# Row sums of 16,384 rows on one core: two blocks of rows for each partition, 112 and 16, laid out as one block of 128

## The chip, the core and the metric

The kernel runs on one core of a Trainium2 chip. The metric is the device time of an execution in microseconds (us). The profile is one execution that was recorded by the hardware profiler; its span runs from its first to its last recorded instruction or transfer.

## The reference

```python
def setup_inputs():
    batch, seq, dim = 32, 512, 1024
    return {"x": np.random.randn(batch, seq, dim).astype(np.float32)}

def reference(x):
    return np.sum(x, axis=-1).astype(np.float32)
```

There are 32 x 512 = 16,384 rows of 1,024 float32 numbers, 4 KB a row and 67.1 MB in all. The output is one float32 sum for each row, 64 KB. Every number is read once and added once.

## The kernel before

The rows are spread over the 128 partitions of the on-chip memory, 128 rows (C) for each partition. They come in two blocks of the input. The first 14,336 rows are the body: partition p has the 112 rows (BODY) that begin at row 112p. The other 2,048 rows are the end: partition p has 16 rows (G) that begin at row 14,336 + 16p. The inner function `block` (lines 27 to 30) makes the views for a block: `x_a` and `out_a` for the body, `x_z` and `out_z` for the end.

The body is loaded in seven steps of 16 rows a partition, 64 KB a partition and 8.39 MB a step, into three buffers `xt` in turn. The end uses the next buffer in turn and comes in pieces of 9, 4 and 2 rows (`CUTS`), and its last row comes in two parts of 544 and 480 columns into a tile of its own, `tail`. All loads are issued by SyncE on one queue, in the order of the list `loads` (lines 128 to 131). From the fourth step on, a load waits until VectorE has finished the step that used the buffer before. The first two loads are moved ahead into the program's entry block (lines 154 to 173); they are one row and fifteen rows of the first step, so that the first step is two DMAs.

VectorE sums 16 rows a step with one tensor_reduce (`rows_dve`, line 55) into `res_a`. In the seventh step it takes nine rows and ScalarE seven, one activation with an accumulator for each row (`rows_act`, line 66). In the end the two engines share the pieces. The last rows are summed on VectorE by instructions that add two halves of a row and accumulate (`pairs_dve`, line 73). The two parts of the last row follow one another, the second one taking up the sum of the first. The sums of the end go to `res_z`.

The results are stored by SyncE on the same queue as the loads. The store of `res_a` (line 135) is issued once the first part of the last row has landed, and the store of `res_z` (line 138) once every sum is there. SyncE then waits for both, clears the semaphores and ends:

```python
    nc.sync.dma_start(out=out_a, in_=res_a[:, :]).then_inc(sems["early_store"], 16)
    nc.sync.wait_ge(vec, count["vec"])
    nc.sync.wait_ge(act, count["act"])
    nc.sync.dma_start(out=out_z, in_=res_z[:, :]).then_inc(sems["store"], 16)
```

Of the kernel before, what the change touches and what calls it, by code (L numbers as in the profile page):

```python
# [9 lines left out]
BODY = 112  # L10
G = 16
# [7 lines left out]
def row_sums(nc, x: bass.AP, out: bass.AP):  # L19
    P = nc.NUM_PARTITIONS  # L20
    x_flat = x.flatten_outer_dims()
    R, D = x_flat.shape
    C = R // P
    assert R % P == 0 and C == BODY + G and BODY % G == 0
    out_flat = out.rearrange("a (b c) -> (a b c)", c=1)

    def block(r0, n):
        x_b = x_flat[r0 : r0 + P * n].rearrange("(p c) d -> p (c d)", p=P)
        out_b = out_flat[r0 : r0 + P * n].rearrange("(p c) -> p c", p=P)
        return x_b, out_b  # L30

    x_a, out_a = block(0, BODY)
    x_z, out_z = block(P * BODY, G)

    def sbuf(name, n):
        return nc.alloc_sbuf_tensor(name, [P, n], F32)
# [47 lines left out]
    for b in range(n_bufs):  # L84
        c = b * G
# [60 lines left out]
def kernel(tc: tile.TileContext, x: bass.AP, out: bass.AP):  # L146
    tc.close()
    tc.compile()  # L148
    nc = tc.nc
    row_sums(nc, x, out)  # L150

    sp = mybir.EngineType.SP
    fn = nc.m.functions[0]
    entry, body = None, None
    for blk in fn.blocks:
        ops = [i for i in blk.instructions if i.engine == sp]
        if entry is None:
            entry = blk  # L160
        elif any(i.opcode == "DMACopy" for i in ops):
            body = blk
            break
    code = list(body.instructions)
    loads = [i for i in code if i.engine == sp and i.opcode == "DMACopy"][:EARLY]
    for load in loads:
        assert not load.sync_info.on_wait
        code.remove(load)
    body.instructions = code
    code = list(entry.instructions)  # L170
    at = next(k for k, i in enumerate(code) if i.engine == sp and i.opcode == "Drain")
    code[at:at] = loads
    entry.instructions = code
# [29 lines left out]
```

## Time and profile before

| | |
|---|---|
| median of 3 runs | 160.55 us (160.54 to 160.86) |
| the profiled execution | 160.55 us |
| its span | 159.2 us |
| VectorE busy | 121.4 us (76% of the span), 16 instructions |
| ScalarE busy | 17.2 us (11%), 31 instructions |
| moved by the DMA queue | 67.18 MB, mean 422 GB/s |
| one reduce of 16 rows a partition | 17.2 us |
| store of `res_a`, 56 KB, issue to landing | 1.6 us |
| store of `res_z`, 8 KB, issue to landing | 1.4 us |

In the profile, DVE is VectorE, ACT is ScalarE, SPq is SyncE's queue of instructions, and "DMA" the 16 DMA engines. L55 is line 55 of the kernel. A part written out<-in names the tensor that is written and the one that is read, `in_x_dram` and `out_dram` being the input and the output in the chip's main memory. The rows of digits cut the span into 40 equal slices, with the busy share of each in tenths. In a timeline, the brackets hold the idle time of the engine before the instruction and what ended it. A packet is one contiguous run that a DMA engine moves, or the closing packet that counts up a semaphore.

### The profile page before, as it was taken

Reading aid. Unit: us, or ns where it says so; the run is one execution under the profiler, and the core shown is the slowest. Engines: PE = TensorE matmul, PEld = TensorE weight load, DVE = VectorE, ACT = ScalarE, POOL = GpSimd, SP = SyncE. Lnnn points to the kernel's source line nnn. Section 1 sums busy time; section 2 is a strip of 40 time slices with the busy share of each in tenths; the row PEclk is TensorE's granted clock in tenths of the full one; section 3 lists DMA queues with packets and bytes.
Section 4 is the critical chain, followed back from the end, with each engine's and each line's share of the span. In section 5 each row is a group of like instructions: output and inputs, shape, how many; then the busy total and the mean of one; then the engine's idle time right before and its main releaser. Section 6 shows DMA issues by size and latency. Waiting matters only on the chain.

```text
span 159.2 us, 107 instructions
## 1 busy us (share of the span) xinstructions
DVE 121.4 (76%) x16; ACT 17.2 (11%) x31; POOL 0.2 (0%) x4
## 2 busy tenths in 40 slices
DVE  0000059997799968999499994999949999499685
ACT  3000000000000000000000000000000000494694
POOL 0000000000000000000000000000000000000000
DMA  9988996996996999979969969969979899699994
GB/s 379 494 370 370 494 527 263 527 527 263 527 494 296 527 395 395 527 313 477 527 263 527 527 263 527 527 263 527 477 313 527 362 428 527 296 445 445 387 400 152
DMA packets 2160, 67.18 MB, mean 422 GB/s; under 512 B 496, under 2 KB 624, under 8 KB 880
## 3 DMA queue, kind: packets, MB, share of 16 engines
q1 hardware_dynamic: 2160, 67.18, 98.1%
HBM read 67.11 MB, written 0.07 MB: 422 GB/s over the span
## 4 chain that ended last, share of the span: by engine, by line
DMA 75%; DVE 22%; SPq 1%; issue 0%
DMA xt<-in_x_dram 50%; DMA tail<-in_x_dram 25%; DVE res_a L55 22%; SPq L131 1%; DVE pairs L73 0%; DVE res_z L73 0%
## 5 line engine op out<-in xcount | busy, mean ns | idle before, releaser
L55 DVE TENSOR_REDUCE res_a<-xt 128x16 f32<-128x16384 f32 (+1 forms) x7 | 113.1, 16153 | 32.3 <-DMA xt<-in_x_dram 32.3
L66 ACT ACTIVATE xt<-xt 128x1024 f32<-128x1024 f32 x15 | 15.6, 1043 | 138.1 <-DMA xt<-in_x_dram 138.1
L55 DVE TENSOR_REDUCE res_z<-xt 128x4 f32<-128x4096 f32 (+1 forms) x2 | 6.7, 3353 | 1.7 <-DMA xt<-in_x_dram 1.7
L66 ACT ACTIVATION_READ_ACCUMULATOR xt<-xt 128x1 f32 x15 | 2.8, 187 | 0.0
L97 DVE MEMSET tail<- 128x1 f32 x1 | 0.1, 59 | 2.0 <-PEq L148 2.0
L66 ACT ACT_TABLE_LOAD x1 | 1.3, 1283 | 1.9 <-PEq L148 1.9
L73 DVE CUSTOM_DVE_ANT_0 pairs<-tail 128x272 f32<-128x272 f32 (+1 forms) x2 | 0.9, 427 | 0.1
L73 DVE CUSTOM_DVE_ANT_0 pairs<-xt 128x512 f32<-128x512 f32 x1 | 0.7, 693 | 0.2 <-DMA xt<-in_x_dram 0.2
L73 DVE DVE_READ_ACCUMULATOR2_ANT res_z<- 128x1 f32 x2 | 0.2, 82 | 0.0
L187 POOL MEMSET const-uint8-127<- 128x1 uint8 x1 | 0.1, 102 | 0.0
L187 POOL MEMSET const-bfloat16-1.0<- 128x1 bf16 x1 | 0.1, 101 | 0.0
L187 POOL MEMSET const-float32-0.0<- 128x1 f32 x1 | 0.1, 98 | 0.2 <-issue 0.2
L187 POOL MEMSET const-float32-1.0<- 128x1 f32 x1 | 0.1, 98 | 0.0
L73 DVE DVE_READ_ACCUMULATOR2_ANT tail<- 128x1 f32 x1 | 0.1, 83 | 0.0
## 6 DMA issues: line engine op xcount, KB each, us to landing
xt<-in_x_dram SPq DMA_DIRECT2D x1, 7680.0 KB, 21.1
xt<-in_x_dram SPq DMA_DIRECT2D x1, 4608.0 KB, 32.4
xt<-in_x_dram SPq DMA_DIRECT2D x1, 2048.0 KB, 36.9
xt<-in_x_dram SPq DMA_DIRECT2D x1, 1024.0 KB, 38.9
xt<-in_x_dram SPq DMA_DIRECT2D x1, 512.0 KB, 3.4
tail<-in_x_dram SPq DMA_DIRECT2D x1, 272.0 KB, 39.1
tail<-in_x_dram SPq DMA_DIRECT2D x1, 240.0 KB, 39.2
xt<-in_x_dram SPq DMA_DIRECT2D x6, 40.8
```

Source lines behind the costliest of these rows:

```text
L55: nc.vector.tensor_reduce(out=res[:, c : c + n], in_=t[:, j * D : (j + n) * D].rearrange("p (j d) -> p j d", d=D), axis=X, op=ADD,).then_i ...
L66: nc.scalar.activation(out=v, in_=v, func=COPY, accum_out=res[:, c + i : c + i + 1]).then_inc(act, 1)
L73: nc.vector.tensor_tensor_reduce(out=pairs[:, 0 : h - a], in0=t[:, a:h], in1=t[:, h:b], scale=1.0, scalar=0.0, op0=ADD, op1=ADD, accum_out ...
L97: nc.vector.memset(tail[:, CUT + 15 : CUT + 16], 0.0).then_inc(vec, 1)
L131: nc.sync.dma_start(out=dst, in_=src).then_inc(s, 16)
L187: nc = _bacc.Bacc("TRN2", target_bir_lowering=False, num_devices=1)
```

## The change

The inner function `block` goes. Partition p has the 128 rows that begin at row 128p. The body is the first 112 of these, the end the last 16. The output is viewed in the same way: the 112 sums of `res_a` are written to the first 112 columns of a view of 128 x 128 sums, and the 16 sums of `res_z` to its last 16 columns. What follows in the code takes the four views as before.

```diff
-    def block(r0, n):
-        x_b = x_flat[r0 : r0 + P * n].rearrange("(p c) d -> p (c d)", p=P)
-        out_b = out_flat[r0 : r0 + P * n].rearrange("(p c) -> p c", p=P)
-        return x_b, out_b
-
-    x_a, out_a = block(0, BODY)
-    x_z, out_z = block(P * BODY, G)
+    x_rows = x_flat.rearrange("(p c) d -> p (c d)", p=P)
+    out_rows = out_flat.rearrange("(p c) -> p c", p=P)
+    x_a, x_z = x_rows[:, 0 : BODY * D], x_rows[:, BODY * D : C * D]
+    out_a, out_z = out_rows[:, 0:BODY], out_rows[:, BODY:C]
```

## The prediction

> **What bounds the kernel now.** I read four views in this order: the slices and queue totals of the page, the chain that ended last, the timeline of the body, and the timeline of the end.
>
> The page's slices and queue totals come first:
>
> ```profile
> span 159.2 us, 107 instructions
> ...
> DVE  0000059997799968999499994999949999499685
> ...
> DMA  9988996996996999979969969969979899699994
> ...
> DMA packets 2160, 67.18 MB, mean 422 GB/s; under 512 B 496, under 2 KB 624, under 8 KB 880
> ...
> q1 hardware_dynamic: 2160, 67.18, 98.1%
> ```
>
> The DMA row has no gap after the start, and the one queue's packets fill 98.1% of the 16 engines' span. VectorE has a hole in nearly every block. So the stream of input sets the pace. The count gives the shape of the transfers: there are 13 loads and 2 stores, and 15 x 128 runs (one for each partition) + 15 x 16 closing packets (one for each engine) = 2160. Each partition's piece is therefore one run already, in both blocks; the stores are 2 x 128 runs, which with the 240 closing packets are the 496 under 512 B.
>
> The chain says the same, with its shares:
>
> ```profile
> DMA 75%; DVE 22%; SPq 1%; issue 0%
> DMA xt<-in_x_dram 50%; DMA tail<-in_x_dram 25%; DVE res_a L55 22%; SPq L131 1%; DVE pairs L73 0%; DVE res_z L73 0%
> ```
>
> The 22% of VectorE are no bound: the chain steps through two reduces only because load b waits until block b-3 is reduced (line 130). Such a load then needs 40.8 us to land (median of the DMA issues), since two whole blocks are queued ahead of it. A block later or earlier on VectorE by less than that does not show.
>
> The timeline of VectorE gives the landing times, because each reduce starts when its block has landed (columns: start, duration, instruction, idle time before it):
>
> ```profile
> 79.65 17.22 DVE L55 TENSOR_REDUCE res_a<-xt 128x16 f32<-128x16384 f32 x1 [2.14 <-DMA xt<-in_x_dram]
> 98.99 17.22 DVE L55 TENSOR_REDUCE res_a<-xt 128x16 f32<-128x16384 f32 x1 [2.12 <-DMA xt<-in_x_dram]
> ...
> 118.34 17.22 DVE L55 TENSOR_REDUCE res_a<-xt 128x16 f32<-128x16384 f32 x1 [2.13 <-DMA xt<-in_x_dram]
> ```
>
> Blocks land 19.34 and 19.35 us apart; the next one, at 137.70, comes 19.36 after. A block is 128 x 64 KB = 8.39 MB, so the rate is 8.39 MB / 19.36 us = 433 GB/s. VectorE is idle 2.13 us of each.
>
> The same view of the end, with the last pieces and the stores:
>
> ```profile
> 137.70 9.75 DVE L55 TENSOR_REDUCE res_a<-xt 128x9 f32<-128x9216 f32 x1 [2.14 <-DMA xt<-in_x_dram]
> ...
> 148.70 4.42 DVE L55 TENSOR_REDUCE res_z<-xt 128x4 f32<-128x4096 f32 x1 [1.25 <-DMA xt<-in_x_dram]
> ...
> 153.56 2.29 DVE L55 TENSOR_REDUCE res_z<-xt 128x2 f32<-128x2048 f32 x1 [0.43 <-DMA xt<-in_x_dram]
> ...
> 156.05 0.69 DVE L73 CUSTOM_DVE_ANT_0 pairs<-xt 128x512 f32<-128x512 f32 x1 [0.21 <-DMA xt<-in_x_dram]
> ...
> 156.72 0.35 SPq L135 DMA_DIRECT2D out_dram<-res_a  x1
> ...
> 157.33 0.41 DVE L73 CUSTOM_DVE_ANT_0 pairs<-tail 128x241 f32<-128x241 f32 x1
> ...
> 157.77 0.34 SPq L138 DMA_DIRECT2D out_dram<-res_z  x1
> ```
>
> The pieces of 9, 4 and 2 rows land 11.00, 4.86 and 2.49 us after what came before; the last row's second half lands at 157.28 (the chain's step in order of time), 1.23 later. After that the end is fixed: 0.05 of issue, 0.41 for the last sum, 0.03 to the store's issue at 157.77, and 1.4 us until it lands, at 159.2.
>
> **The base of the sum.** The profiled execution took 160.55 us, its span is 159.2, and 1.35 lies around it. The median of the three runs is 160.55 too, so the sum needs no correction.
>
> **Part 1: instructions.** None is added, removed or moved. The reduces, activations, waits, semaphores, buffers and the issue order of the one queue stay as they are, and every slice still has 128 rows of one run each: 9 rows of a partition were contiguous and still are. So engines' work costs 0, and the packet count should stay 2160.
>
> **Part 2: the distance between partitions in the input.** A row of x is 4 KB. In the block of 112 rows a partition's neighbour lies 112 x 4 = 448 KB further; in the block of 16, 16 x 4 = 64 KB. Both become 128 x 4 = 512 KB. All that the change can do to the 154.9 us of loading (67.1 MB at 433 GB/s) is through these addresses. The trace has no load at 512 KB, so I bound it from both sides.
>
> The nearest row is the only other power of two in the trace, the 64 KB of the last block. Its 16 rows take 157.28 - 137.70 = 19.58 us, against 19.36 for 16 rows at 448 KB: 0.22 us or 1.1% more. Two causes fit that. One is the distance: all partitions start at the same place in a 64 KB grid, so the 16 engines, which run side by side, ask for like addresses at once. The other is that this block is five DMAs and the other one, at 0.055 us for each of the four more. By the pieces: 9 rows should take 9/16 of 19.36 = 10.89 and take 11.00 (+1.0%), 4 rows 4.84 and take 4.86 (+0.4%), 2 rows 2.42 and take 2.49 (+2.9%).
>
> Lower bound: if all of the 0.22 is the price of the four DMAs, the distance costs nothing. It can go below nothing by a little: if 64 KB was what cost the 0.22, and 512 KB is as good as 448, the block gets it back, -0.2. More is excluded by the 98.1% share: the queue has no gaps to close. Upper bound: the worst of the larger pieces, 2.9%, on all eight blocks is 8 x 19.36 x 0.029 = +4.5. The value I take is the 64 KB block as a whole, since it is the nearest row in kind: seven blocks by 0.22 = +1.5, and the last block as it is. I take the distance rather than the DMA count because the piece with the most bytes, 9 rows, bears half of the 0.22 alone (0.11), which a fixed price for each DMA does not give (the 4 rows bear 0.02).
>
> The Trainium skill has a rule that speaks against this change: "DMA: Bandwidth & Descriptors", in its section "Latency and other measured facts", lists copies of 128-partition tiles at large powers of two between partitions, with 207 GB/s for each direction at 512 KiB where 214 is full, much less at 2 and 4 MiB, and full rate again with 4 KiB more between partitions. As an estimate from that page the loads would take 214/207 = 1.034 of their time, some +5.2 us or 165.8 in all. Its copies read and write HBM at once, and this kernel only reads until its end; no row of this trace shows a load at 512 KiB, and the sum above goes without it.
>
> Where a stall goes: a block that lands 0.22 later finds VectorE idle 2.13 already, so its idle time becomes 2.35, and nothing on VectorE, ScalarE or the queue moves to the path. The load of block b is still issued about two blocks ahead of its data. The delay adds up along the queue, and the last row's landing moves by the whole of it, from 157.28 to about 158.8.
>
> **Part 3: the stores.** The last store (line 138) wrote 128 runs of 64 B end to end; now the runs lie 512 B apart, each behind 448 B of the early store (line 135), which is issued 1.05 us before it and lands after 1.6, at 158.3. The last one is on the path with its full 1.4. The nearest rows are these two: 1.4 where the runs are small and 1.6 where they are large and not end to end with other data in flight. So +0.2 if scattered runs cost as the larger ones do, or if the second store's writes are held behind the first one's in the same 512 B. No reason excludes a gain of the same kind, 0.1 say. The number of runs is the same, and I take 0. The early store is covered: line 142 waits for it only 0.2 us, at a time when the last store is still under way; with that cover gone it would cost as much.
>
> Sum: 160.55 + 0 + 1.5 + 0 = 162.05; I write 162.0.
>
> **Rivals.** *The engines set the rate, not the addresses.* The queue's share of 98.1%, and the same 433 GB/s in block after block, speak for engines at their own limit; memory then has room to spare, and a like start for all partitions does not show. Against it stands the 0.11 of the 9-row piece. This ends at 160.55, with 160.35 to 160.75 by the stores and the 0.2: no change that can be measured, since about 0.2% (0.32 us) is what a measurement of this kernel can tell from none. It decides if the memory can deliver over 433 GB/s at 512 KB.
>
> *The last block gains.* The 64 KB distance was the bad one, 512 KB is as good as 448, and the store gains its 0.1: 160.55 - 0.22 - 0.1 = 160.2, just faster. For it: the excess sits in the 64 KB block alone. Against it: 64 KB and 512 KB are both powers of two, and it needs two small gains at once.
>
> *The distance costs more than the nearest row.* At 2.9% it is +4.5, 165.05, and with +0.2 at the store 165.3. For it: 512 KB is a coarser grid than 64 KB, so more address bits agree among the engines. Against it: the 2-row piece is short, and a fixed price weighs most in it.
>
> That the change does not do what it says is not open here: the slices are plain, and the addresses are all that differs.
>
> **How the numbers follow.** The distance costs, between 160.9 and 165.3 with the likeliest at 162.0: 0.62, of which 0.2 is for the costlier rival near 165. The engines set the rate: 0.28. The last block gains: 0.10. So slower 0.62, same 0.28, faster 0.10. The range takes in all cases from 160.2 to 165.3; what is left out is the costlier rival's part above and a gain below, together 2 in 10 at most. The forecast's own case alone is 160.9 to 163.5.
>
> **What would show it.** Right: 2160 packets; blocks landing 19.5 to 19.7 us apart; idle time before each reduce at about 2.35; the last row at 158.8; the last store at 1.4. The engines' rival: 19.36 apart as before. The costlier one: 19.9, with idle times near 2.7. The forecast is wrong in kind if the blocks keep their 19.36 and the time still moves, by the stores or the last pieces; or if the packet count changes, which would mean that the runs were cut otherwise.

## The result, and the profile after

In 11 executions of each, the changed kernel took 161.22 us (median; 161.01 to 161.43) and the kernel before 160.79 us (160.54 to 161.25). The ratio is 1.0027 with a 95% interval of 1.0017 to 1.0036: slower by 0.43 us. The forecast was 162.0, which is 1.45 us above the 160.55 that the prediction started from. The direction is right and the forecast size is over three times too large.

The profiled execution took 161.23 us with a span of 159.9, so it stands near its median. The one of before, with 160.55, is among the quickest of its kernel. The two traces therefore differ by 0.68 us where the medians differ by 0.43, and up to a quarter of a microsecond between them is scatter.

The page's head, slices and queue totals:

```profile
span 159.9 us, 107 instructions
...
DMA  9979996997969969969969979979989799699994
...
DMA packets 2160, 67.18 MB, mean 420 GB/s; under 512 B 496, under 2 KB 624, under 8 KB 880
...
q1 hardware_dynamic: 2160, 67.18, 98.0%
```

The packets are the same in number and in size classes, and the queue is as full as before. The transfers have the same shape.

The timeline of VectorE (start, duration, instruction, idle time before it):

```profile
22.05 17.22 DVE L52 TENSOR_REDUCE res_a<-xt 128x16 f32<-128x16384 f32 x1 [20.01 <-DMA xt<-in_x_dram]
41.46 17.22 DVE L52 TENSOR_REDUCE res_a<-xt 128x16 f32<-128x16384 f32 x1 [2.19 <-DMA xt<-in_x_dram]
61.01 17.22 DVE L52 TENSOR_REDUCE res_a<-xt 128x16 f32<-128x16384 f32 x1 [2.32 <-DMA xt<-in_x_dram]
80.39 17.22 DVE L52 TENSOR_REDUCE res_a<-xt 128x16 f32<-128x16384 f32 x1 [2.17 <-DMA xt<-in_x_dram]
99.72 17.22 DVE L52 TENSOR_REDUCE res_a<-xt 128x16 f32<-128x16384 f32 x1 [2.11 <-DMA xt<-in_x_dram]
119.07 17.22 DVE L52 TENSOR_REDUCE res_a<-xt 128x16 f32<-128x16384 f32 x1 [2.13 <-DMA xt<-in_x_dram]
138.43 9.75 DVE L52 TENSOR_REDUCE res_a<-xt 128x9 f32<-128x9216 f32 x1 [2.13 <-DMA xt<-in_x_dram]
149.34 4.42 DVE L52 TENSOR_REDUCE res_z<-xt 128x4 f32<-128x4096 f32 x1 [1.16 <-DMA xt<-in_x_dram]
```

Each start is a landing. In the trace of before the first three steps landed here:

```profile
21.66 17.22 DVE L55 TENSOR_REDUCE res_a<-xt 128x16 f32<-128x16384 f32 x1 [19.62 <-DMA xt<-in_x_dram]
40.93 17.22 DVE L55 TENSOR_REDUCE res_a<-xt 128x16 f32<-128x16384 f32 x1 [2.05 <-DMA xt<-in_x_dram]
60.29 17.22 DVE L55 TENSOR_REDUCE res_a<-xt 128x16 f32<-128x16384 f32 x1 [2.14 <-DMA xt<-in_x_dram]
```

The fourth landed at 79.65. Now the four are late by 0.39, 0.53, 0.72 and 0.74 us. From there on nothing is added: the steps land 19.33, 19.35 and 19.36 us apart, as they did at 448 KB, and the delay at 138.43 is still 0.73. The trace of before is a quick one, though. Against out_only below, which has the same loads as before and lands its first steps at 21.89, 41.16, 60.52 and 79.87, the delays are 0.16, 0.30, 0.49 and 0.52. Either way the loss of this execution is in the first three steps, and from the fourth on a step at 512 KB costs no more than one at 448.

The 9-row piece takes 149.34 - 138.43 = 10.91 us, where the trace of before had 11.00. The last data land at 157.95, 0.67 later than before, by the chain in order of time (start, duration, step):

```profile
118.76 39.19 DMA tail<-in_x_dram
157.95 0.05 issue
```

And the stores, from the view of the DMA issues (KB, then us to landing):

```profile
out_dram<-res_a SPq DMA_DIRECT2D x1, 56.0 KB, 1.5
out_dram<-res_z SPq DMA_DIRECT2D x1, 8.0 KB, 1.4
```

The last store takes 1.4 us as before, the early one 1.5 in place of 1.6. The end is not where the time went.

The trace file also holds a record of every single packet, which the views above only sum up. A record gives the start, the duration and the size but no engine. The engines are read from it as 16 chains: each long run begins within about 0.01 us of the end of the one before it on its engine, but for a few where chains cross. A 64 KB run of one partition takes 2.418 us (after) and 2.420 us (before) in the median, which for 16 engines is 433 to 434 GB/s: the same pace at either distance. Of the 128 runs of 60 KB that make up the rest of the first step, 5 took over 2.29 us in the trace of before, with a longest of 2.42 (the median is 2.27). In the trace after it is 19, with a longest of 2.62, and 18 of these are the first or second run of their engine. The second, third and fourth steps after have 34, 30 and 16 runs of 64 KB (of 128 each) that took over 2.44 us, the fifth and sixth none; in the trace of before the second step has one and the next three have none.

### The profile page after: what moved, and what is told of

It reads as the page before. It is cut to its first block, busy times and chain, and to the rows that moved or that the text cites. A ratio compares the mean times of both kernels' runs of the same rounds, so it can differ in the third digit from the quotient of the medians.

```text
span 159.9 us, 107 instructions
## 1 busy us (share of the span) xinstructions
DVE 121.4 (76%) x16; ACT 17.2 (11%) x31; POOL 0.2 (0%) x4
## 2 busy tenths in 40 slices
DMA packets 2160, 67.18 MB, mean 420 GB/s; under 512 B 496, under 2 KB 624, under 8 KB 880
## 3 DMA queue, kind: packets, MB, share of 16 engines
q1 hardware_dynamic: 2160, 67.18, 98.0%
## 4 chain that ended last, share of the span: by engine, by line
DMA 75%; DVE 22%; SPq 1%; issue 0%
DMA xt<-in_x_dram 50%; DMA tail<-in_x_dram 25%; DVE res_a L52 22%; SPq L128 1%; DVE pairs L70 0%; DVE res_z L70 0%
```

## Theories

*T1, like starts.* The 16 engines begin at the same moment at addresses that are multiples of one distance apart, and at 512 KB they hinder one another until each has got a different lag; then all run at their own pace, and the last one keeps its lag to the end. *The stores* are the rival on the other end of the kernel, and *every step* is the forecast's own. *T3, cold start:* only what is first after the launch is dear; it was put as a rival with step0_448. *T4, the small load:* the addresses of the one-row load that opens the stream decide, whatever follows; it was put as a rival with row0_448.

## Experiments

Each median stands against the kernel before on the same chip, with a 95% interval of the ratio. The diffs show the lines that matter; most lines that only define a view are left out. `x_rows` and `out_rows` are the views of input and output as one block of 128 rows a partition, and `x_s` is the view whose distance is tried.

**Loads alone and stores alone (in_only, out_only).**

```diff
 in_only, against the kernel before:
     x_a, out_a = block(0, BODY)
     x_z, out_z = block(P * BODY, G)
+    x_a, x_z = x_rows[:, 0 : BODY * D], x_rows[:, BODY * D : C * D]
 out_only, in the same place:
+    out_a, out_z = out_rows[:, 0:BODY], out_rows[:, BODY:C]
```

> Only the loads use one block of 128 rows a partition; the stores stay as in the kernel before, so the sums land in the places of other rows. Theory of the start (T1): with 512 KB between partitions the 16 engines begin side by side at like addresses, hinder one another in the first three steps until they have drifted apart, and run at the old pace after that; the stores cost nothing. Expected: +0.4 to +0.7 us against the kernel before, first step landing at about 22.0, fourth at about 80.4, then 19.35 us a step. Rival (stores): the loss is in the stores; then this run equals the kernel before, within 0.2. Rival (distance at every step): then 19.5 us or more at every step.

> Only the stores are columns of one block of 128; the loads stay as in the kernel before, so the sums land in the places of other rows. T1: no difference, within 0.15 us. Rival (stores): +0.4 us, and the last store takes longer than 1.4 us to land.

Loads alone: 161.39 against 160.81, ratio 1.0032 (1.0022 to 1.0042), the whole of the loss and, by the medians, a little more (0.58 us against 0.43, with intervals that overlap). Stores alone: 160.74, ratio 0.9997 (0.9989 to 1.0006). The stores are out, and so is *every step*: in the trace of in_only the steps after the first land 19.33 to 19.37 us apart. The first one landed at 22.14, in an execution of 161.03, among the quickest of its kernel.

**The first step alone (step0_512, step0_448).** The first kernel is the one before with only its first step at 512 KB; the second is the one after with only its first step at 448 KB.

```diff
+            src = x_s if b == 0 else x_a
-            loads.append((b, xt[b % BUFS][:, i * D : j * D], x_a[:, (c + i) * D : (c + j) * D], s))
+            loads.append((b, xt[b % BUFS][:, i * D : j * D], src[:, (c + i) * D : (c + j) * D], s))
```

> The kernel before, but the first step alone (its 16 rows of a partition) is read with 512 KB between partitions; so some rows are read twice and some never. T1: the conflict is at the start, where the engines are side by side, so most of the loss is there: first step at about 22.0, in all +0.3 to +0.5 us. Rival (each 512 KB step pays its share, +0.43/8): +0.05 us, not to be told from nothing.

> The kernel after, but the first step alone is read with 448 KB between partitions; so some rows are read twice and some never. T1 in the form 'engines side by side': 448 KB leaves them nearly side by side, so the conflict only moves to the second step: first step at 21.66, the next two each 0.1 to 0.4 longer than 19.35, in all +0.3 to +0.7. Rival (a cold start: the first touches of memory are what 512 KB makes dearer): the loss is gone, 0 to +0.1.

step0_512 took 161.29 against 160.81, ratio 1.0026 (1.0015 to 1.0037): one step of eight at 512 KB brings the whole loss. step0_448 took 160.82, ratio 0.9998 (0.9989 to 1.0007): seven steps of eight at 512 KB bring none once the first is at 448. The second result is a miss for T1 as it was put, and what the cold start expected. VectorE's timeline in step0_512:

```profile
22.44 17.22 DVE L56 TENSOR_REDUCE res_a<-xt 128x16 f32<-128x16384 f32 x1 [20.40 <-DMA xt<-in_x_dram]
41.72 17.22 DVE L56 TENSOR_REDUCE res_a<-xt 128x16 f32<-128x16384 f32 x1 [2.06 <-DMA xt<-in_x_dram]
61.08 17.22 DVE L56 TENSOR_REDUCE res_a<-xt 128x16 f32<-128x16384 f32 x1 [2.13 <-DMA xt<-in_x_dram]
```

The first landing is at 22.44, and what follows goes at the old pace. The packet records of this run have 26 stretched runs (over 2.29 us) in the first step, up to 3.04 us, and 19 of them are the first or second of their engine. In step0_448 the first and seventh landings are these:

```profile
22.00 17.22 DVE L53 TENSOR_REDUCE res_a<-xt 128x16 f32<-128x16384 f32 x1 [19.95 <-DMA xt<-in_x_dram]
...
138.02 9.76 DVE L53 TENSOR_REDUCE res_a<-xt 128x9 f32<-128x9216 f32 x1 [2.13 <-DMA xt<-in_x_dram]
```

Its six steps between them, all at 512 KB, take 19.34 us on average, so the extra time of the second and third steps of the kernel after is absent here. That extra time, too, hangs on how the stream starts.

**Seven more starts (restart_448, restart_512).** T1 and the cold start part here: if it is the start from rest that costs, it must cost again at each one.

```diff
+        if b in (1, 2, 3, 4, 5, 6, 7) and b not in seen:
+            seen.add(b)
+            nc.sync.wait_ge(slots[(b - 1) % BUFS], 16 * ((b - 1) // BUFS + 1))
         nc.sync.dma_start(out=dst, in_=src).then_inc(s, 16)
```

> The kernel before, with one wait more ahead of the first load of each step from the second on (seven places): the load is issued only once the step before it has landed, so that all 16 engines start again side by side each time. This run is the base for the next one. Each restart should cost the time from issue to first byte and from last byte to the semaphore, about 2 us, so some +12 to +16 us; steps land about 21.3 us apart.

> The kernel after with the same seven waits. Theory side by side (T1, mended after the runs before: a step read at 448 KB already leaves the engines far enough apart): every restart repeats the conflict, so against the other run with waits each of the steps takes 0.2 to 0.5 us longer, in all +1.5 to +3.5 us. Theory cold start (T3): only what is first after the launch is dear, so the difference stays at +0.4 to +0.6 us, all of it in the first step.

They took 178.89 and 182.36 us; the difference is 3.47 where without restarts it is 0.43. Each restart costs 2.6 us in restart_448, more than the 2 expected. Its first six are at 448 KB; the seventh opens the last block, which that kernel reads at 64 KB. VectorE's timeline, first three steps of restart_448:

```profile
22.12 17.22 DVE L55 TENSOR_REDUCE res_a<-xt 128x16 f32<-128x16384 f32 x1 [20.07 <-DMA xt<-in_x_dram]
43.88 17.22 DVE L55 TENSOR_REDUCE res_a<-xt 128x16 f32<-128x16384 f32 x1 [4.54 <-DMA xt<-in_x_dram]
65.71 17.22 DVE L55 TENSOR_REDUCE res_a<-xt 128x16 f32<-128x16384 f32 x1 [4.61 <-DMA xt<-in_x_dram]
```

and of restart_512:

```profile
22.52 17.22 DVE L52 TENSOR_REDUCE res_a<-xt 128x16 f32<-128x16384 f32 x1 [20.48 <-DMA xt<-in_x_dram]
44.82 17.22 DVE L52 TENSOR_REDUCE res_a<-xt 128x16 f32<-128x16384 f32 x1 [5.08 <-DMA xt<-in_x_dram]
67.16 17.22 DVE L52 TENSOR_REDUCE res_a<-xt 128x16 f32<-128x16384 f32 x1 [5.13 <-DMA xt<-in_x_dram]
```

The seventh step lands at 153.60 and at 156.64. So six steps take (153.60 - 22.12) / 6 = 21.91 and (156.64 - 22.52) / 6 = 22.35 us: 0.44 more for each start at 512 KB, and 0.40 for the first. The cold start falls. A start from rest at 512 KB costs 0.4 us more than one at 448, not once but on the average of all starts; single ones scatter, and the difference runs from 0.09 to 0.68 us in the six steps.

The seventh restart of restart_448 is a start from rest at 64 KB. Its 9-row piece lands 167.26 - 153.60 = 13.66 us after the step before, 2.74 more than the 10.92 of a running stream (out_only). In restart_512 the same takes 170.72 - 156.64 = 14.08, which is 3.17 more than 10.91 (after). One start in one execution is little, but there 64 KB stands nearer to the 2.6 of 448 KB than to 512.

**Other distances (p508, p256, restart_508, s0_64, p64).** They ask whether the power of two is what matters. `wide` is the number of rows that a partition has in a block.

```diff
 p508: all but the last row from a block of 127 rows, the last from one of 1 row
+    x_a, x_z = x_w[:, 0 : BODY * D], x_w[:, BODY * D : wide * D]
 p256 and p64: every step from blocks of 64 or of 16 rows
+    x_n = x_flat.rearrange("(k p c) d -> k p (c d)", p=P, c=wide)
 s0_64: the first step from a block of 16 rows, the rest from one of 112
+    x_0 = x_flat[0 : P * G].rearrange("(p c) d -> p (c d)", p=P)
+    x_r = x_flat[P * G : R].rearrange("(p c) d -> p (c d)", p=P)
```

> The kernel before with 508 KB between partitions in the body and in the last block but its last row, which comes from a block of one row a partition (the stores stay as before, so the sums land in the places of other rows). If the power of two is what costs: the first step lands at about 21.7 to 22.0 as before, in all 0 to +0.15 us. If mere distance or the span of addresses costs: +0.4 as at 512 KB.

> The kernel before with the input in two blocks of 64 rows a partition, so 256 KB between partitions in every load (the stores stay as before, so the sums land in the places of other rows). If the price comes with the number of like address bits, it is half of that at 512 KB or less: +0.1 to +0.25 us, in the first step. If every large power of two is alike: +0.4. If only 512 KB is hit: 0.

> The kernel with 508 KB between partitions (last row and stores as told there) with the seven restarts. Its base is the kernel before with restarts, 178.89 us; at 512 KB it was 182.36. If mere distance or the span of the addresses costs at each start: about 182.0 to 182.5. If the power of two costs and the 0.39 us of the run without restarts came from the small first load (4 KB a partition) alone: 178.7 to 179.6.

> The two blocks of the kernel before in the other order: the first step's 16 rows from a block of 16 rows a partition (64 KB), the seven others from a block of 112 (448 KB); stores as before, so the sums land in the places of other rows. T1 says that only the start counts. If a start at 64 KB is free, this equals the kernel before or wins the 0.1 us that its 9-row piece at 64 KB costs it: -0.15 to +0.05 us. If 64 KB hinders a start as 512 KB does: +0.3 to +0.5, in the first step.

> The input in eight blocks of 16 rows a partition, 64 KB between partitions in every load, so each step reads 8.39 MB end to end; stores as before, so the sums land in the places of other rows. T1: at most the start differs: -0.15 to +0.5 us with the same first step as the run with the first step alone at 64 KB, and 19.35 us a step after it. Rival (a power of two costs at every step while engines stand alike): 19.4 to 19.6 us a step, +0.4 to +1.7 us.

| distance | run | us | before | ratio (95%) |
|---|---|---|---|---|
| 508 KB | p508 | 161.12 | 160.73 | 1.0020 (1.0011 to 1.0029) |
| 256 KB | p256 | 160.78 | 160.73 | 1.0011 (1.0000 to 1.0022) |
| 64 KB first, then 448 | s0_64 | 161.37 | 160.79 | 1.0035 (1.0022 to 1.0048) |
| 64 KB | p64 | 161.49 | 160.79 | 1.0044 (1.0032 to 1.0057) |
| 508 KB with restarts | restart_508 | 182.01 | 160.79 | 1.1318 (1.1298 to 1.1338) |

The power of two falls as the cause: 508 KB is none and costs nearly what 512 KB does, with restarts too (182.01 against 182.36, though in the profiled execution of restart_508 one single step took 23.30 us, where the other five took 21.88 to 22.39). But the size of the distance isn't it either, since the smallest, 64 KB, costs no less than 512. The mere order of the two blocks matters: 16 rows last is the kernel before, 16 rows first costs 0.6 us. In the profiled executions of s0_64 and p64 the first step lands at 22.36 and 22.67, and the other steps of the body follow 19.27 to 19.37 us apart, so the loss at 64 KB is at the start too; p64, whose profiled execution is the slowest of its own, loses another 0.3 us in its 9-row piece. By the medians 448 KB does best among the distances tried, and 256 KB is next to it.

p256 is the one run whose loss lies wholly away from the start. Its executions scatter from 160.58 to 161.39, and the profiled one is the slowest of them. Its VectorE timeline:

```profile
21.79 17.22 DVE L63 TENSOR_REDUCE res_a<-xt 128x16 f32<-128x16384 f32 x1 [19.75 <-DMA xt<-in_x_dram]
41.08 17.22 DVE L63 TENSOR_REDUCE res_a<-xt 128x16 f32<-128x16384 f32 x1 [2.07 <-DMA xt<-in_x_dram]
60.80 17.22 DVE L63 TENSOR_REDUCE res_a<-xt 128x16 f32<-128x16384 f32 x1 [2.50 <-DMA xt<-in_x_dram]
80.36 17.22 DVE L63 TENSOR_REDUCE res_a<-xt 128x16 f32<-128x16384 f32 x1 [2.34 <-DMA xt<-in_x_dram]
```

The first two steps are quick, and the next two take 19.72 and 19.56 us. In that execution 60, 48 and 52 of the 128 runs of the third, fourth and fifth steps took over 2.44 us. So a stream can lose time after its start too; why it did so here is not shown.

**The small first load (row0_448, row0_512, p508_row0, nofirst_448, nofirst_512).** The stream opens with one row of each partition, then come the other 15. The first reduce waits for all 16, so the small load feeds nothing earlier. The runs named row0 change the distance of this load alone; p508_row0 is p508 with it at 448 KB. The runs named nofirst load the first step as one, so one load instead of two stands in the entry block, and VectorE's wait for the small load goes.

```diff
 row0_448 (on the kernel after), row0_512 (on the kernel before):
+            src = x_s if b == 0 and j == 1 else x_a
 nofirst_448 (on the kernel before), nofirst_512 (on the kernel after):
-        parts = [(0, G, slots[b % BUFS])] if b else [(0, 1, sems["first"]), (1, G, slots[0])]
+        parts = [(0, G, slots[b % BUFS])]
```

> The kernel after, but the first row alone (the small first load, 4 KB a partition) is read with 448 KB between partitions, so one row of each partition is another partition's. The profile after shows the stretched transfers at 512 KB among the first two runs of each engine in the load of 15 rows, not in the small one. T1: the loss stays, +0.3 to +0.5 us, first step at about 22.0 to 22.4. Rival (the small first load sets how the engines stand to one another, and 512 KB spoils that): 0 to +0.1.

> The kernel before, but the first row alone (the small first load) is read with 512 KB between partitions, so one row of each partition is another partition's. Theory of the small load (T4: its addresses set how the engines stand to one another when the long runs begin, whatever follows): +0.3 to +0.5 us. Theory of like starts (T1: a conflict needs 512 KB in the long runs too): 0 to +0.1, since the 15 rows are at 448 KB.

> The kernel with 508 KB between partitions, but the small first load at 448 KB; rows and stores otherwise as told there. T4: the loss of 0.39 us is gone, 0 to +0.1. T1 in any form that needs the long runs to collide: it stays, +0.3 to +0.4.

> The kernel before without the small first load: the first step is one load of 16 rows (and one load instead of two stands in the entry block). No reduce gains by the small load, since the first one waits for all 16 rows. T4: the small load breaks up the side-by-side start with cheap 4 KB runs; without it the first long runs stretch as after the restarts (steps there took about 0.4 to 0.9 us more than 21.3), +0.3 to +1.0 us. If the small load does nothing: -0.1 to +0.1.

> The kernel after without the small first load. Both theories of a conflict among long runs that start side by side: above the 448 KB run without the small load by 0.3 to 0.6 us, as at each restart (3.47 us over eight starts, 0.43 each). If only the small load bore the price of 512 KB: equal to the 448 KB run within 0.15.

| small load | the rest | run | us | before | ratio (95%) |
|---|---|---|---|---|---|
| 448 KB | 512 KB | row0_448 | 160.81 | 160.79 | 1.0004 (0.9995 to 1.0013) |
| 512 KB | 448 KB | row0_512 | 161.01 | 160.77 | 1.0014 (1.0005 to 1.0023) |
| 448 KB | 508 KB | p508_row0 | 161.01 | 160.77 | 1.0013 (1.0004 to 1.0021) |
| none | 448 KB | nofirst_448 | 160.76 | 160.77 | 0.9995 (0.9986 to 1.0003) |
| none | 512 KB | nofirst_512 | 161.40 | 160.77 | 1.0034 (1.0021 to 1.0047) |

With its small load at 448 KB the kernel after loses nothing, against what T1 expected; its packet records have only 2 stretched runs. With the small load at 512 KB the kernel before loses 0.24 us, between what the two theories expected. Neither is right alone: as long as a small load opens the stream, the whole loss needs both parts at 512 KB, and the small load alone brings about half. For 508 KB a small load at 448 lowers the median loss from 0.39 to 0.24 us, but the intervals overlap, so no cure is shown. T4 falls as a whole rule. What remains of T1 is that the start decides, through whatever the engines read first; that like addresses hinder one another there is not shown.

The packet records show that the last engine falls behind in two ways. Times are from the first packet, for the engine that begins the second step last:

| run | its long runs begin (us) | its first long run takes (us) |
|---|---|---|
| out_only (no loss) | 2.30 | 2.27 |
| step0_448 (no loss) | 2.42 | 2.27 |
| step0_512 | 2.11 | 3.04 |
| in_only | 1.96 | 2.91 |
| after | 2.15 | 2.60 |
| p508 | 2.74 | 2.27 |
| row0_512 | 2.56 | 2.27 |
| p508_row0 | 2.51 | 2.27 |

With both parts at 512 KB it starts its long runs in time, and the first of them is stretched. With 508 KB, or with the small load alone at 512, its long runs are as quick as ever, but the small load lets it go late. T1 spoke of the first way only.

The pair without a small load shows the start most plainly, as only runs of 64 KB are there. In nofirst_448 the packet records have all 16 engines begin their first run within 0.35 us, each run taking 3.06 to 3.48 us; the second runs begin within 0.56 us of one another. In nofirst_512 the engines begin one after another, spread over 1.46 us, with first runs of 2.42 to 3.32 us, and the second runs begin over 1.00 us. The whole of the two kernels differs by 0.64 us. Their VectorE timelines, first and seventh landing, for 448 KB:

```profile
21.89 17.22 DVE L55 TENSOR_REDUCE res_a<-xt 128x16 f32<-128x16384 f32 x1 [20.33 <-DMA xt<-in_x_dram]
...
137.98 9.75 DVE L55 TENSOR_REDUCE res_a<-xt 128x9 f32<-128x9216 f32 x1 [2.13 <-DMA xt<-in_x_dram]
```

and for 512 KB:

```profile
22.43 17.22 DVE L52 TENSOR_REDUCE res_a<-xt 128x16 f32<-128x16384 f32 x1 [20.86 <-DMA xt<-in_x_dram]
...
138.52 9.76 DVE L52 TENSOR_REDUCE res_a<-xt 128x9 f32<-128x9216 f32 x1 [2.13 <-DMA xt<-in_x_dram]
```

They are 0.54 apart at the first landing and 0.54 apart at the seventh. What the last engine loses at the start is neither made up nor added to in this pair.

One number from the packet records puts the profiled executions in order: the time from the first packet to the moment when the last of the 16 engines begins its run of the second step.

| run | last engine begins step 2 (us) | that execution (us) |
|---|---|---|
| before | 20.22 | 160.55 |
| p256 | 20.37 | 161.39 |
| row0_448 | 20.39 | 160.69 |
| out_only | 20.41 | 160.74 |
| nofirst_448 | 20.53 | 160.80 |
| step0_448 | 20.55 | 160.84 |
| after | 20.60 | 161.23 |
| p508_row0 | 20.62 | 160.91 |
| row0_512 | 20.67 | 160.94 |
| in_only | 20.72 | 161.03 |
| p508 | 20.85 | 161.12 |
| s0_64 | 20.95 | 161.20 |
| step0_512 | 21.01 | 161.29 |
| nofirst_512 | 21.03 | 161.30 |
| p64 | 21.24 | 161.79 |

The order of the two columns agrees but for two: p256, whose loss comes in its third to fifth steps, and the kernel after, which in that execution loses another 0.33 us in its second and third steps. No kernel here was faster than the one before beyond its interval.

## Why the prediction was wrong

**The direction** was right: slower, through the addresses of the loads. But the sum reached it by a price for each step that isn't there, so the right direction was partly luck. That no instruction changes, that the packets stay 2160, and that the stores cost nothing were right as well: out_only shows no loss, and the last store still takes 1.4 us.

**The step that failed** is in part 2: the 0.22 us that the last block took more than a body block were read as the price of 64 KB between partitions, and were then put on each of seven steps, +1.5. The runs show what they were. In the profile after, the last block has no 64 KB any more and still takes 157.95 - 138.43 = 19.52 us, some 0.17 more than a step. In out_only, which reads it at 64 KB, it takes 157.45 - 137.92 = 19.53. So the distance has no part in most of the excess. The block's four more DMAs, at 0.04 each, are the prediction's other reading and fit, though no run changed their number alone. And the 0.11 of the 9-row piece, which made me choose the distance, was scatter:

```profile
137.92 9.76 DVE L57 TENSOR_REDUCE res_a<-xt 128x9 f32<-128x9216 f32 x1 [2.13 <-DMA xt<-in_x_dram]
148.84 4.42 DVE L57 TENSOR_REDUCE res_z<-xt 128x4 f32<-128x4096 f32 x1 [1.17 <-DMA xt<-in_x_dram]
```

out_only reads that piece at 64 KB too, and it takes 148.84 - 137.92 = 10.92, where 11.00 was read and 10.89 would be 9/16 of a step. One execution gave me a difference of 0.1 us, and it was not there in the next. The price of 512 KB on a step of the running stream is nothing: 19.33 to 19.36 from the fifth step on in the profile after, and 19.34 on average in step0_448.

**The term that was missing** is the start. The prediction spoke of the engines asking for like addresses at once, but costed it as a rate. It is a lag that is paid once for each start, about 0.4 us, and that the last engine carries to the end. So the marks that the prediction named are absent in nearly every step: it put the steps 19.5 to 19.7 apart, the idle time before each reduce at 2.35 and the last row at 158.8, where the profile has 19.35, 2.13 and 157.95. Only the third step looks like them (19.55, idle 2.32). What came is near the prediction's sign of being wrong in kind, blocks that keep their 19.36 while the time moves, but by the start, which it did not list.

**The rival** that the engines set the rate was right about the body, where it was given 0.28, and missed the start as well. The costlier case at 2.9% a step is far off, and so is the last block's gain: that block takes 19.52 us at 512 KB and 19.53 at 64. The Trainium skill's row ("DMA: Bandwidth & Descriptors", section "Latency and other measured facts"), 207 in place of 214 GB/s at 512 KiB, does not show here: reads of 64 KB runs at 512 KB go at 433 to 434 GB/s in the median, as they do at 448. Its copies, which write memory too and in shorter runs, were not tried.

**The base** was 160.55, a median of three that lay 0.24 below the median of eleven. The executions of one kernel scatter by 0.71 us from end to end, more than the effect.

**What stays open** is which property of the addresses decides. In front of a whole stream 448 KB starts well, 256 KB nearly so, and 64, 508 and 512 KB do not; neither the power of two nor the size sorts them. Why the small load runs late in some cases and the first long run in others is open too. How memory maps these addresses can't be seen in these runs.

## What to carry to other kernels

When one queue is full from start to end, split the price of an address pattern in two before multiplying: a rate, which every step pays, and a lag from the start, which the slowest engine pays once for each start from rest. A difference of 0.1 us between two rows of one profile is no price per step until a second execution shows it. And a stream that must be restarted often pays the start's price each time: here 2.6 us at 448 KB between partitions, and 0.44 more on average at 512.

## What was not expected of the hardware

The last DMA engine does not catch up: its lag stood through the later steps (in the packet records after, the last engine's start trails the first one's by 0.57 us in each of the fifth to seventh steps). At a start from rest at 448 KB all engines' first runs of 64 KB take about 3.2 us in place of 2.42 (nofirst_448), while at 512 KB they begin one after another over 1.46 us (nofirst_512). The small load that opens the kernel before buys nothing that can be measured (0.9995, 0.9986 to 1.0003).
